# Expert choice one chunk behind its queries, the gate table in 32-token blocks, and other rates for the gathered rows

## The chip, the cores and the metric

The kernel runs on one core of one Trainium2 chip. A core has engines that run side by side and wait for one another by semaphores: PE (TensorE, matmuls, with its weight loads PEld), DVE (VectorE), ACT (ScalarE), POOL (GpSimd) and SP (SyncE); 16 DMA engines carry data between DRAM and the on-chip memory. The metric is the device time of one execution in microseconds (us). Before the change it is 4591.96 us, the median of 3 runs (4589.6 to 4595.62).

## The reference

One layer of a bidirectional encoder on 512 tokens of width 2048, all in float32:

```
h = rms_norm(x); proj = h @ w_in          # 2048 x 19456, split into nine parts
ret = retention(...) @ w_ret_out          # 8 heads, both directions
att = dilated_window_attention(...) @ w_attn_out
x = x + (sigmoid(gate_ret) * ret + sigmoid(gate_att) * att) @ w_out
h2 = rms_norm(x)
x = x + peer_ffn(h2)

# peer_ffn: 8 heads, 2 x 128 keys, 16384 experts of one neuron, 16 of them for each token and head
q = h2 @ w_query                          # 2048 x 2048
s1, s2 = q's two halves against the head's two sets of 128 keys
v1, i1 = top_k(s1, 16); v2, i2 = top_k(s2, 16)
best, pos = top_k(v1[:, None] + v2[None, :], 16)      # over 256 sums
expert = i1[pos // 16] * 128 + i2[pos % 16]; gate = softmax(best)
out = sum over the 128 chosen of gelu(h2 . u[expert]) * gate * v[expert]
```

## The kernel before

Each product of float32 operands is made of three matmuls: every operand is split into a high part (ACT casts it: whi, uh, vh, wh) and a low part (DVE subtracts: wlo, ul, vl, wl). `load_w` (lines 121 to 134) does this for weights: SP loads two slabs of 128 x 512 (`wraw`, four buffers), ACT makes `whi`, DVE `wlo` (three buffers each). `gemm` (lines 136 to 149) runs over such loads for a chunk of 512 output columns.

The 512 tokens are four tiles of 128. Tile 0 is mixed and routed first (part 0), tiles 1 to 3 afterwards (part 1). `mixers` makes retention and attention, `merge` (line 546) the two output projections, `w_out`, the residual x1 and its norm h2. At the end of `merge`, for each of four chunks of 512 columns and each tile, SP loads the input's piece `xr` (three buffers), DVE adds it to the product in x1, SP writes that to DRAM (`x1D`), and ACT squares it for the norm. Then x1 is scaled, PE transposes it, and h2 is split once more. The norm's gains `fgr` are loaded into the same three buffers as xr.

`routing` (line 634) has four chunks of two heads. In a chunk PE makes the queries, transposes them and multiplies them with the transposed keys `skT`; ACT copies the scores to `s12s`; DVE then selects: five instructions for each of 12 rows of scores (MAX, MAX_INDEX, MATCH_REPLACE and two more, in `top16`), the best of 50 sums, and the indices and gates out of them, some 114 instructions for three tiles. `routing_tables` (line 715) loads the keys with their two inner axes swapped and transposes them on PE.

The experts are used in two ways. For tiles 0 and 1 each token's rows are gathered (a unit of 256 steps: 128 rows of u, one for each of a token's choices, then 128 of v). A step is one indirect DMA of 1 MB on POOL's queue (`gr`, three buffers) and one DVE instruction over 128 x 2048 (line 765 or 774). Steps are dealt out by `tick(anchor, rate)`: the rate is added to a credit, and each whole credit uses one row and issues another after the anchor instruction. For tiles 2 and 3 (256 tokens) all 16384 experts are computed. They are 128 blocks of 128, in the code and here called experts for short: `expert_in(n)` (48 matmuls of 256 columns, weights `ur` loaded and split by `load_u`) and `expert_out` (products with v into `psy`). Between the two the activations are multiplied by a dense table of gates.

The table of gates, 128 x 128 experts by 256 tokens, is built on chip from one-hot vectors: for eight tokens DVE makes `oh2` and part of `oh1`, ACT scales four of oh1 by the gates, PE multiplies them (`gg`), ACT copies the products to `Gs`. A block of 64 tokens is 4 MB and goes to DRAM (`GD`); there are four blocks. Later `gate_tile` reads back two experts' gates for all tokens.

The order after the second merge: routing of three tiles, with `begin_dense` (the first 11 experts, `NFIRST`) put before the last chunk's selection; the transposes of the choices (`hkT`) and their way over DRAM; the table, with 12 experts spread over its blocks and one behind; then 16 steps in which only `expert_out` runs, since 24 experts (`NPRE`) are already there; then steps with one `expert_in` and one `expert_out` each. Rows are gathered at a rate of 1.0 for each eight tokens of the table, at 0.7 (`early_rate`) in the first 24 output steps, and at what is left over in the remaining 96.

The order of instructions on each engine is not the order of the code: a scheduler places them ahead of time by the code's order as a priority and by when it estimates operands to be there. Each engine and each queue then runs its list strictly in order.

## Time and profile before

| | |
|---|---|
| median of 3 runs | 4591.96 us |
| profiled execution | 4602.08 us, span 4600.3 us |
| mean granted TensorE clock | 0.967 of full speed |
| PE busy | 4211.8 us (92%) |
| DVE busy | 3439.3 us (75%) |
| ACT, POOL busy | 1917.0 us, 795.5 us |
| moved by DMA | 1358.78 MB, mean 295 GB/s |

The span runs from the first to the last instruction. A busy share is a mean over stages that have different limits, so the rows below go by stages. Matmuls are pipelined and their ends are modelled. A bracket behind a row of a timeline is the idle time of that engine before the instruction, and what ended it. PEclk is the granted clock as a share of 2.4 GHz.

### The profile page before, as it was taken

How to read it: one execution, taken by the hardware profiler on the slowest of the kernel's cores; microseconds unless marked ns; L12 is line 12 of the kernel's file. 1: busy time of each engine (PE TensorE's matmuls, PEld its weight loads, DVE VectorE, ACT ScalarE, POOL GpSimd, SP SyncE). 2: the span in 40 equal slices, each digit the busy share in tenths (PEclk: the TensorE clock that was granted, in tenths of full speed). 3: DMA queues.
4: the chain of work that ended last, by engine and by line, in shares of the span. 5: the costliest groups of instructions: out<-in, count | busy, mean ns of one | idle time of the engine just before them, and what ended most of it. 6: DMA issues, size and time to landing. Idle time of an engine off the chain costs nothing.

```text
span 4600.3 us, 57918 instructions
## 1 busy us (share of the span) xinstructions
PE 4211.8 (92%) x21638; PEld 3524.4 (77%) x21638; DVE 3439.3 (75%) x4495; ACT 1917.0 (42%) x2674; POOL 795.5 (17%) x516
## 2 busy tenths in 40 slices
PE   8999998988998999989979977886799999999999
PEld 6878776765776778767758866786689998899997
DVE  7454554546566878677678878888779998999997
ACT  6444555545442323443432333344434443344443
POOL 0000000000002112222122221012112332344332
PEclk9999999999999999999989998998899999999999
DMA  7666675758658889888899885267889999999997
GB/s 241 226 219 218 215 243 178 244 193 287 224 160 303 323 290 331 313 305 320 300 346 373 340 323 202 92 236 292 318 302 363 397 400 391 401 400 402 405 403 293
DMA packets 510171, 1358.78 MB, mean 295 GB/s; under 512 B 49216, under 2 KB 129088, under 8 KB 440768
## 3 DMA queue, kind: packets, MB, share of 16 engines
q1 hardware_dynamic: 432800, 816.00, 50.9%
q0 software_dynamic: 73728, 536.90, 29.7%
q8 instruction: 170, 2.79, 0.2%
q10 hardware_dynamic: 3360, 2.17, 0.2%
q14 instruction: 113, 0.93, 0.1%
HBM read 1290.05 MB, written 64.88 MB: 295 GB/s over the span
## 4 chain that ended last, share of the span: by engine, by line
PE 50%; DMA 18%; DVE 13%; issue 13%; ACT 3%; POOL 2%; SPq 0%; ACTq 0%; DVEq 0%; POOLq 0%
PE gB L147 9%; PE gB L148 9%; PE gB L146 9%; PE psy L981 3%; PE psy L982 3%; PE psy L980 3%; PE psa L856 3%; PE psa L854 3%; PE psa L855 3%; DMA gr<-in_peer_v,eid 3%; DMA ur<-in_u_feat 3%; DMA wraw<-in_w_in 2%; POOL gr L756 2%; DVE wlo L131 2%; DMA vr<-in_peer_v 2%
## 5 line engine op out<-in xcount | busy, mean ns | idle before, releaser
L131 DVE TENSOR_TENSOR wlo<-wraw,whi 128x1024 fp32r<-128x1024 f32 x752 | 917.2, 1223 | 650.6 <-ACT whi L130 636.0
L130 ACT CAST whi<-wraw 128x1024 fp32r<-128x1024 f32 x752 | 789.4, 1051 | 1227.7 <-PE gB L148 913.6
L756 POOL DMA_INDIRECT gr<-in_peer_u,eid x256 | 362.9, 1418 | 2752.8 <-DVE eid L743 1535.1
L774 DVE SCALAR_TENSOR_TENSOR accg<-gr,wg,accg 128x2048 f32<-128x2048 f32 x256 | 600.5, 2346 | 50.6 <-DMA gr<-in_peer_v,eid 38.5
L765 DVE SCALAR_TENSOR_TENSOR gr<-gr,hrow 128x2048 f32<-128x2048 f32 x256 | 583.8, 2284 | 45.7 <-DMA gr<-in_peer_u,eid 44.2
L854 PE MATMUL psa<-rh,uh 128*128 128x256 f32 x2048 | 582.1, 284 | 29.6 <-ACT uh L839 29.6
L756 POOL DMA_INDIRECT gr<-in_peer_v,eid x256 | 432.4, 1689 | 994.8 <-DVE accg L774 929.1
L856 PE MATMUL psa<-rh,ul 128*128 128x256 f32 x2048 | 581.8, 284 | 9.8 <-DVE ul L840 9.8
L855 PE MATMUL psa<-rl,uh 128*128 128x256 f32 x2048 | 580.0, 283 | 0.0
L839 ACT CAST uh<-ur 128x1024 fp32r<-128x1024 f32 x256 | 268.9, 1051 | 479.0 <-DMA ur<-in_u_feat 381.1
L981 PE MATMUL psy<-vl,wh 128*128 128x512 f32 x1024 | 405.1, 396 | 19.7 <-DVE vl L974 19.5
L854 PEld LDWEIGHTS psa<-rh,uh 128*128 128x128 f32 x2048 | 390.9, 191 | 34.7 <-ACT uh L839 30.5
L980 PE MATMUL psy<-vh,wh 128*128 128x512 f32 x1024 | 402.5, 393 | 6.0 <-ACT vh L973 5.9
L982 PE MATMUL psy<-vh,wl 128*128 128x512 f32 x1024 | 400.7, 391 | 0.0
L855 PEld LDWEIGHTS psa<-rl,uh 128*128 128x128 f32 x2048 | 397.6, 194 | 4.0
L856 PEld LDWEIGHTS psa<-rh,ul 128*128 128x128 f32 x2048 | 390.7, 191 | 12.2 <-DVE ul L840 12.0
L973 ACT CAST vh<-vr 128x1024 fp32r<-128x1024 f32 x256 | 267.9, 1050 | 300.6 <-DMA vr<-in_peer_v 164.5
L974 DVE TENSOR_TENSOR vl<-vr,vh 128x1024 fp32r<-128x1024 f32 x256 | 310.4, 1220 | 76.8 <-ACT vh L973 76.4
L147 PE MATMUL gB<-wlo,rh 128*128 128x512 f32 x768 | 316.3, 412 | 52.3 <-DVE wlo L131 52.0
L840 DVE TENSOR_TENSOR ul<-ur,uh 128x1024 fp32r<-128x1024 f32 x256 | 311.2, 1218 | 57.5 <-ACT uh L839 56.3
L146 PE MATMUL gB<-whi,rh 128*128 128x512 f32 x768 | 309.2, 406 | 31.5 <-ACT rh L570 22.7
L148 PE MATMUL gB<-whi,rl 128*128 128x512 f32 x768 | 311.0, 405 | 0.3 <-DVE rl L571 0.2
(467 smaller groups left out, 7957.5 us busy)
## 6 DMA issues: line engine op xcount, KB each, us to landing
wraw<-in_w_in SPq DMA_DIRECT2D x528, 512.0 KB, 5.0
ur<-in_u_feat SPq DMA_DIRECT2D x256, 512.0 KB, 9.6
vr<-in_peer_v SPq DMA_DIRECT2D x256, 512.0 KB, 9.9
wraw<-in_w_ret_out SPq DMA_DIRECT2D x64, 512.0 KB, 6.1
wraw<-in_w_out SPq DMA_DIRECT2D x64, 512.0 KB, 5.8
wraw<-in_peer_w_query SPq DMA_DIRECT2D x64, 512.0 KB, 4.9
wraw<-in_w_attn_out SPq DMA_DIRECT2D x32, 512.0 KB, 6.8
GD<-Gs SPq DMA_DIRECT2D x4, 4096.0 KB, 14.6
```

What stands on the lines that cost most here:

```text
L130: nc.scalar.copy(whi, raw)
L131: low = nc.vector.tensor_sub(wlo, raw, whi.bitcast(F32))
L146: nc.tensor.matmul(ps[t], ah(k), whi[:, j], start=first, stop=False)
L147: nc.tensor.matmul(ps[t], ah(k), wlo[:, j], start=False, stop=False)
L148: nc.tensor.matmul(ps[t], al(k), whi[:, j], start=False, stop=last)
L756: nc.gpsimd.indirect_dma_start(out=r, out_offset=None, in_=pu if s < P else pv_, in_offset=bass.IndirectOffsetOnAxis(ap=u.eid[:, s % P:s % ...
L765: nc.vector.scalar_tensor_tensor(r, r, 1.0, u.hrow, op0=ALU.mult, op1=ALU.mult, accum_out=u.ag[:, s:s + 1])
L774: nc.vector.scalar_tensor_tensor(u.acc, r, u.wg[:, s - P:s - P + 1], u.acc, op0=ALU.mult, op1=ALU.add)
L854: nc.tensor.matmul(psa[:, j], uh[:, cs], chi[k], start=k == 0, stop=False)
L855: nc.tensor.matmul(psa[:, j], uh[:, cs], clo[k], start=False, stop=False)
L856: nc.tensor.matmul(psa[:, j], ul[:, cs], chi[k], start=False, stop=k == KT - 1)
L981: nc.tensor.matmul(ps[:, t], wh[:, j, ts_], vl[:, j], start=False, stop=False)
```

## The change

`merge` adds the residual into xr itself, writes xr to DRAM, lets ACT square it into x1 and then copy it to x1. `routing` is cut in two: `queries(c)` makes the scores of a chunk, `select(c, scs)` chooses; chunk c's selection follows the queries of chunk c + 1, and the first experts (`before_last`) now come between the last queries and the last two selections. The score tiles have eight buffers for four. The keys are laid out on the host and loaded with one DMA. The scratch tile `ef` goes. The table's blocks are 32 tokens (`TB`), eight of them, with two buffers for Gs; 16 experts come before the table and 7 are spread over it; rows are gathered at 0.6 for each eight tokens of the table and at 1.1 in the first 24 output steps. A gate tile holds four experts.

```diff
--- before.py
+++ after.py
@@ -607,9 +607,10 @@
             for t in range(T):
                 xr = mg.tile([P, 512], F32, name="xr", tag="xr", bufs=3)
                 nc.sync.dma_start(xr, x4[t0 + t][:, cs])
-                nc.vector.tensor_add(x1[t][:, cs], ps[t], xr)
-                nc.sync.dma_start(x1D[t0 + t][:, cs], x1[t][:, cs])
-                nc.scalar.activation(xr, x1[t][:, cs], AF.Square, accum_out=ss4[:, t, c:c + 1])
+                nc.vector.tensor_add(xr, ps[t], xr)
+                nc.sync.dma_start(x1D[t0 + t][:, cs], xr)
+                nc.scalar.activation(x1[t][:, cs], xr, AF.Square, accum_out=ss4[:, t, c:c + 1])
+                nc.scalar.copy(x1[t][:, cs], xr)
         fg = mg.tile([P, KT], F32, name="ffng")
         nc.sync.dma_start(fg, I["ffn_norm_g"][0].rearrange("(k p) -> p k", p=P))
         for t in range(T):
@@ -634,13 +635,12 @@
 
         N2 = 2 * T
         gates, e1, e2 = [rt.tile([P, T, 8, 16], F32, name=n, bufs=1) for n in ("gates", "e1", "e2")]
-        for c in range(4):
+        def queries(c):
+
             ps = paired((I["peer_w_query"][0], c * 512, tiles2))
             qn = rt.tile([P, T, 512], F32, name="qn", bufs=2)
             for t in range(T):
                 nc.scalar.copy(qn[:, t], ps[t])
-            v12 = rt.tile([P, T, 2, 2, 16], F32, name="v12")
-            i12 = rt.tile([P, T, 2, 2, 16], U32, name="i12")
             scs = []
             for i in range(4):
                 pt = bank("qT")
@@ -652,11 +652,14 @@
                 for t in range(T):
                     nc.tensor.matmul(ss[:, t * P:(t + 1) * P], qT[:, t * P:(t + 1) * P], skT[:, 4 * c + i],
                                      start=True, stop=True)
-                sc = rt.tile([P, T * P], F32, name="s12s", bufs=4)
+                sc = rt.tile([P, T * P], F32, name="s12s", bufs=8)
                 nc.scalar.copy(sc, ss[:, :T * P])
                 scs.append(sc)
-            if c == 3 and before_last:
-                before_last()
+            return scs
+
+        def select(c, scs):
+            v12 = rt.tile([P, T, 2, 2, 16], F32, name="v12")
+            i12 = rt.tile([P, T, 2, 2, 16], U32, name="i12")
             for i in range(4):
                 for t in range(T):
                     scr = rt.tile([P, P], F32, name="scr")
@@ -710,19 +713,22 @@
             nc.vector.tensor_mul(gates.rearrange("p t (c u) k -> p t c u k", c=4)[:, :, c],
                                  ex.rearrange("p (t u) k -> p t u k", t=T),
                                  sm.rearrange("p (t u) -> p t u", t=T)[:, :, :, None].to_broadcast([P, T, 2, 16]))
+
+        found = {}
+        for c in range(4):
+            found[c] = queries(c)
+            if c == 3 and before_last:
+                before_last()
+            if c > 0:
+                select(c - 1, found.pop(c - 1))
+        select(3, found.pop(3))
         return e1, e2, gates
 
     def routing_tables(rt):
         tab = rt.tile([P, 3, 16], F32, name="tab", bufs=1)
         nc.sync.dma_start(tab.rearrange("p a b -> p (a b)"), bcast(I["c_rank"], 48))
         skT = rt.tile([P, 16, P], F32, name="skT", bufs=1)
-        for q4 in range(4):
-            sk = rt.tile([P, 4, P], F32, name="sk", bufs=1)
-            nc.sync.dma_start(sk, I["peer_sub_keys"][0].rearrange("h s k d -> k (h s) d")[:, 4 * q4:4 * q4 + 4])
-            ps = bank("skT")
-            for i in range(4):
-                nc.tensor.transpose(ps[:, i * P:(i + 1) * P], sk[:, i], ident)
-            nc.scalar.copy(skT[:, 4 * q4:4 * q4 + 4].rearrange("p a b -> p (a b)"), ps)
+        nc.sync.dma_start(skT, I["key_feat"].rearrange("d (a k) -> d a k", a=16))
         return skT, tab
 
 
@@ -738,9 +744,8 @@
         u.t = t
         u.eid = ga.tile([P, P], I32, name=f"eid{t}")
         u.gate = ga.tile([P, P], F32, name=f"gate{t}")
-        ef = ga.tile([P, P], F32, name="ef", tag="ef")
-        nc.vector.scalar_tensor_tensor(ef, flat(e1), float(P), flat(e2), op0=ALU.mult, op1=ALU.add)
-        nc.vector.tensor_copy(u.eid, ef)
+        nc.vector.scalar_tensor_tensor(u.gate, flat(e1), float(P), flat(e2), op0=ALU.mult, op1=ALU.add)
+        nc.vector.tensor_copy(u.eid, u.gate)
         nc.vector.tensor_copy(u.gate, flat(gates))
         u.h2 = h2row
         gstate["todo"] += [(u, s) for s in range(2 * P)]
@@ -814,13 +819,13 @@
 
     TG = 2
     ND = TG * P
-    TB = 64
+    TB = 32
     NB = ND // TB
     NE = 2
     NV = 8
     NGRP = P // NV
     NPRE = 24
-    NFIRST = 11
+    NFIRST = 16
     NLAST = 1
     right = ctx.enter_context(ExitStack())
     pools = {}
@@ -902,7 +907,7 @@
         for blk in range(NB):
             for n in range(*[NFIRST + (NPRE - NLAST - NFIRST) * (blk + i) // NB for i in (0, 1)]):
                 expert_in(n)
-            Gs = gb.tile([P, P, TB], F32, name="Gs")
+            Gs = gb.tile([P, P, TB], F32, name="Gs", bufs=2)
             for o in range(TB // OB):
                 t0 = blk * TB + o * OB
                 cols = lambda v: v[:, t0:t0 + OB, None].to_broadcast([P, OB, P])
@@ -924,7 +929,7 @@
                         nc.tensor.matmul(ps[:, i * P:(i + 1) * P], oh2[:, j], oh1[:, j], start=True, stop=True)
                     j0 = o * OB + 4 * q
                     nc.scalar.copy(Gs[:, :, j0:j0 + 4], ps.rearrange("p (t e) -> p e t", t=4))
-                tick(last, 1.0)
+                tick(last, 0.6)
             nc.sync.dma_start(GD[blk], Gs)
         for n in range(NPRE - NLAST, NPRE):
             expert_in(n)
@@ -938,15 +943,17 @@
 
     W = {}
 
-    def gate_tile(m):
-        Gt = d2.tile([P, NB, NE * TB], F32, name="Gt")
-        nc.sync.dma_start(Gt, GD[:, :, NE * m:NE * (m + 1), :].rearrange("b p e t -> p b (e t)"))
+    NG = 4
+
+    def gate_tile(i):
+        Gt = d2.tile([P, NB, NG * TB], F32, name="Gt")
+        nc.sync.dma_start(Gt, GD[:, :, NG * i:NG * (i + 1), :].rearrange("b p e t -> p b (e t)"))
         return Gt
 
     def weigh(m, Gt):
         ge = A_out.pop(m)
         gv = ge.rearrange("p j (b t) -> p b j t", t=TB)
-        nc.vector.tensor_mul(gv, gv, Gt.rearrange("p b (j t) -> p b j t", t=TB))
+        nc.vector.tensor_mul(gv, gv, Gt.rearrange("p b (j t) -> p b j t", t=TB)[:, :, m % 2 * NE:(m % 2 + 1) * NE])
         wh = d2.tile([P, NE, ND], F32R, name="wh", bufs=7)
         wl = d2.tile([P, NE, ND], F32R, name="wl", bufs=7)
         nc.scalar.copy(wh, ge)
@@ -954,7 +961,7 @@
         W[m] = (wh, wl)
 
     G0 = NPRE // NV
-    early_rate = 0.7
+    early_rate = 1.1
     left_steps = [(NGRP - 1 - G0) * 8]
 
     def expert_out(g, i):
@@ -998,8 +1005,8 @@
         for q in range(NV):
             n = NV * g + q
             if n < P:
-                if n % NE == 0:
-                    Gt = gate_tile(n // NE)
+                if n % NG == 0:
+                    Gt = gate_tile(n // NG)
                 if n >= NPRE:
                     expert_in(n)
                 if n % NE == NE - 1:
@@ -1018,6 +1025,8 @@
     host = {n: np.ascontiguousarray(inputs[n]) for n in _INS}
     u = host["peer_u"].reshape(P, P, KT, P)
     host["u_feat"] = np.ascontiguousarray(u.transpose(0, 3, 2, 1)).reshape(P, P, KT * P)
+    keys = host.pop("peer_sub_keys").reshape(2 * H, P, P)
+    host["key_feat"] = np.ascontiguousarray(keys.transpose(2, 0, 1)).reshape(P, 2 * H * P)
     host.update(shape_constants())
     return host
```

The first place at which the order changes is SP's queue in the second merge, from the third chunk of `w_out` to the fourth (x1D is the residual in DRAM, DMAHW3_49 and the like are the landing of an earlier DMA of the same queue, Activation_49 and DVE_49 are ACT and DVE). Before:

```order
L611 DMA x1D<-x_0_19291 128x512 [waits DMAHW6_49,DVE_49]
L611 DMA x1D<-x_1_19292 128x512 [waits DVE_49]
L609 DMA xr<-in_x 128x512 [waits Activation_49] x2
L611 DMA x1D<-x_2_19293 128x512 [waits DMAHW2_49,DVE_49]
L127 DMA wraw<-in_w_out 128x2x512 [waits DMAHW3_49,DVE_49]
L609 DMA xr<-in_x 128x512 [waits DMAHW4_49,Activation_49]
L127 DMA wraw<-in_w_out 128x2x512 [waits DMAHW5_49,DVE_49]
```

The same place now:

```order
L611 DMA x1D<-xr 128x512 [waits DMAHW3_49,DVE_49]
L611 DMA x1D<-xr 128x512 [waits DVE_49]
L609 DMA xr<-in_x 128x512 [waits DMAHW3_49,Activation_49]
L611 DMA x1D<-xr 128x512 [waits DVE_49]
L127 DMA wraw<-in_w_out 128x2x512 [waits DMAHW7_49,DVE_49]
L609 DMA xr<-in_x 128x512 [waits DMAHW4_49,DMAHW0_49]
L609 DMA xr<-in_x 128x512 [waits DMAHW6_49,DMAHW1_49,Activation_49]
L127 DMA wraw<-in_w_out 128x2x512 [waits DMAHW2_49,DVE_49]
```

The loads of xr waited for ACT alone or for a DMA eight places back; now each waits for the landing of a write of x1D as well, and the third write and the weight loads stand behind the first of these waits.

The second place is DVE in the second routing, at the weight splits of the second chunk. Before, the end of the first chunk's selection and the first split behind it:

```order
L522 MATCH_REPLACE scr_20861<-best,cand 128x50
L683 COPY di<-i12f 128x6
L684 TENSOR_TENSOR di<-i12f 128x6x15
L523 MAX best<-scr_20861 128x8
L131 TENSOR_TENSOR wlo<-wraw,whi 128x1024
L524 MAX_INDEX pos<-best,scr_20861 128x8
L706 TENSOR_TENSOR ex<-best 128x96
L686 CAST pf<-pos 128x96
```

Now, in the midst of the first chunk's selection (v and i are the values and indices of the first 16):

```order
L524 MAX_INDEX i_20969<-v_20968,scr 128x8
L131 TENSOR_TENSOR wlo<-wraw,whi 128x1024
L779 SCALAR_TENSOR_TENSOR accg<-gr,wg,accg 128x2048
L522 MATCH_REPLACE scr<-v_20968,s12s 128x128
L520 MAX v_20968<-s12s 128x8
L131 TENSOR_TENSOR wlo<-wraw,whi 128x1024
L779 SCALAR_TENSOR_TENSOR accg<-gr,wg,accg 128x2048
L523 MAX v_20968<-scr 128x8
L521 MAX_INDEX i_20969<-v_20968,s12s 128x8
```

Before, 99 instructions of a selection stood ahead of the next chunk's fourth split; now 32 do, and the splits of a chunk are spread through the selection of the chunk before it.

The third place is DVE at the second routing's end. Before, the last split of the last chunk and the start of its selection, whose other instructions then alternate with the first experts' ul:

```order
L703 TENSOR_REDUCE e_20478<-mu 128x3x32
L131 TENSOR_TENSOR wlo<-wraw,whi 128x1024
L520 MAX v_21903<-s12s 128x8 x2
L521 MAX_INDEX i_21904<-v_21903,s12s 128x8
L522 MATCH_REPLACE scr<-v_21903,s12s 128x128
```

Now, 85 instructions of the third chunk's selection behind the last split:

```order
L689 CAST pf<-pos 128x96
L520 MAX v_22911<-s12s 128x8
L698 TENSOR_TENSOR th<-pf,tab 128x1536
L845 TENSOR_TENSOR ul<-ur,uh 128x1024
L699 TENSOR_TENSOR mu<-th,tab 128x1536
L845 TENSOR_TENSOR ul<-ur,uh 128x1024 x2
L700 TENSOR_REDUCE jr<-mu 128x96
```

The end of the third selection and all of the fourth now lie beside the first experts, where the fourth alone did.

## Rows read from the trace of the kernel before

**Rows 1.** Page, parts 1 and 2: PE's share, and granted clock in 40 slices

```profile
PE 4211.8 (92%) x21638; PEld 3524.4 (77%) x21638; DVE 3439.3 (75%) x4495; ACT 1917.0 (42%) x2674; POOL 795.5 (17%) x516
...
PEclk9999999999999999999989998998899999999999
```

**Rows 2.** Stages: length; PE, PEld, DVE, ACT, POOL busy; clock; DMA share; GB/s

```profile
2623.00:2729.00 106.00, 100.95 (x434) 80.85 (x432) 77.25 (x53) 30.88 (x42) 26.70 (x20) 1.00 0.95 360
2729.00:2751.00 22.00, 2.21 (x9) 1.38 (x9) 12.80 (x16) 7.02 (x13) 3.55 (x3) 0.60 0.88 336
...
2797.00:2967.00 170.00, 133.60 (x592) 105.12 (x590) 150.82 (x553) 47.59 (x71) 11.70 (x8) 0.90 0.33 119
2967.00:3032.00 65.00, 62.49 (x530) 61.92 (x531) 58.97 (x178) 30.53 (x34) 1.68 (x1) 0.97 0.58 198
3046.00:3254.00 208.00, 142.29 (x1029) 135.47 (x1028) 181.78 (x273) 100.55 (x220) 51.21 (x31) 0.84 0.72 278
3254.00:3281.00 27.00, 17.92 (x118) 17.23 (x118) 7.72 (x9) 4.87 (x7) 1.14 (x1) 0.81 1.00 377
3281.00:3366.00 85.00, 75.91 (x316) 59.34 (x316) 70.72 (x71) 33.16 (x37) 10.56 (x9) 0.96 0.93 331
3460.00:4560.00 1100.00, 1085.24 (x6968) 986.89 (x6968) 1030.83 (x826) 445.09 (x484) 396.40 (x207) 1.00 1.01 394
```

**Rows 3.** Waits of PE, 2729 to 2797: total us, times, longest

```profile
PE mT L597 <- DVE x L623: 18.3, 2, 16.4
PE skT L724 <- DMA sk<-in_peer_sub_keys: 6.4, 3, 4.4
```

**Rows 4.** DVE's timeline: start and length, then the scaling of x1

```profile
2744.03 1.29 DVE L623 TENSOR_SCALAR x<-x,ssx 128x2048 f32<-128x2048 f32 x1 [4.81 <-DMA x1D<-x]
2749.07 1.29 DVE L623 TENSOR_SCALAR x<-x,ssx 128x2048 f32<-128x2048 f32 x1 [3.75 <-DMA wraw<-in_peer_w_query]
```

**Rows 5.** Waits of PE, 2797 to 2967

```profile
PE gB L147 <- DVE wlo L131: 33.7, 6, 9.3
```

**Rows 6.** The table's writes (line 928): us from issue to landing

```profile
DMA to landing us min/median/max: 13.8/14.6/16.0
```

**Rows 7.** ACT's timeline: a copy of 512 columns; first scores of two chunks

```profile
2798.61 0.59 ACT L641 COPY qn<-gB 128x512 f32<-128x512 f32 x1 [0.32 <-PE gB L148]
...
2804.42 0.48 ACT L656 COPY s12s<-s 128x384 f32<-128x384 f32 x1 [1.15 <-PE s L653]
...
2962.86 0.48 ACT L656 COPY s12s<-s 128x384 f32<-128x384 f32 x1 [1.02 <-PE s L653]
```

**Rows 8.** DMA, 2620 to 2750: POOL's queue; issues, KB, us to landing

```profile
q0 software_dynamic: 3584, 26.08, 50.3%
...
x1D<-x SPq DMA_DIRECT2D x12, 256.0 KB, 11.9
```

**Rows 9.** Waits of PE, 985 to 1020 (first merge)

```profile
PE skT L724 <- DMA sk<-in_peer_sub_keys: 10.6, 3, 8.5
```

**Rows 10.** DVE by line, 2797 to 3046: busy us, mean ns | idle before

```profile
L131 DVE TENSOR_TENSOR wlo<-wraw,whi 128x1024 fp32r<-128x1024 f32 x23 | 27.8, 1212 | 8.1 <-ACT whi L130 8.1
L774 DVE SCALAR_TENSOR_TENSOR accg<-gr,wg,accg 128x2048 f32<-128x2048 f32 x8 | 18.8, 2347 | 1.6 <-DMA gr<-in_peer_v,eid 1.6
```

**Rows 11.** DVE by line, 3046 to 3254

```profile
L765 DVE SCALAR_TENSOR_TENSOR gr<-gr,hrow 128x2048 f32<-128x2048 f32 x29 | 66.1, 2283 | 6.4 <-DMA gr<-in_peer_u,eid 5.1 <-DMA hrow<-h2D 1.3
...
L840 DVE TENSOR_TENSOR ul<-ur,uh 128x1024 fp32r<-128x1024 f32 x21 | 25.1, 1219 | 19.8 <-ACT uh L839 19.8
```

**Rows 12.** The reads of gate tiles (line 943): us to landing

```profile
DMA to landing us min/median/max: 4.1/8.9/12.6
```

**Rows 13.** Waits of PE, 3460 to 4560

```profile
PE psy L981 <- DVE vl L974: 12.1, 9, 5.0
PE psa L856 <- DVE ul L840: 2.5, 1, 2.5
```

## The prediction

> **What bounds the kernel now.** I read the page first: PE is busy for 92% of the span, and its clock row falls below full speed only around slices 17 to 29 [rows 1]. Then I cut the span into stages [rows 2]. The last long one, 3460 to 4560 us, has PE at 1085.2 of 1100 us at the full clock (2.4 GHz): PE sets its time there, and DVE (1030.8) and the DMA engines (share 1.01) have next to nothing to spare [rows 2]. What is slack lies between 2729 and 3281 us. In the first stretch PE does 2.2 us of work in 22 [rows 2]; it waits for the scaled residual [rows 3], which waits for the residual's own write to DRAM [rows 4]. Then come the transposed keys: PE waits 6.4 us for their loads [rows 3]. From 2797 to 2967 DVE is busy 150.8 of 170 us, PE 133.6 [rows 2], and all that PE waits for there is wlo, 33.7 us [rows 5]: the second half of each weight split stands on DVE behind a chunk's whole selection. From 3046 to 3254 (the gate table) DVE is busy 181.8 of 208 us and PE 142.3 at a granted clock of 0.84 [rows 2]: DVE sets the pace. From 3254 to 3281 the last 4 MB of the table go to DRAM and come back [rows 2, 6]. So PE sets the time, except where DVE holds it back in two stretches and a DMA in three.
>
> All sums stand against the profiled execution: span 4600.3 us, 4602.1 us with what lies around it. The median of the runs shown is 4592.0, that is 10.1 less; I carry the difference over to it.
>
> **Residual and squares (merge).** The add now writes xr, which goes to DRAM itself, and x1 is a second copy. DVE's scaling no longer waits for the write: 4.8 and 3.75 us go (the second is put down to a weight load, but the tile's own write is still out) [rows 4]. Into the chain come the ACT copies, three of 512 columns, 0.59 us by the like copy [rows 7], 1.8 in all. That is -8.6 + 1.8 = **-7**, ends -9 and 0. The price stands on SP: xr is loaded again from a ring of three, and that load now waits for the landing of the residual's write, with the next weight loads behind it on the queue; the third write is itself behind the first wait. I count seven such landings in series, one after the first chunk and two after each of the other three. One landing takes 11.9 us here [rows 8], so the bound is 83 us. The other end is 0: half of the bytes in this stretch are rows on POOL's own queue [rows 8], the engines are at a share of 0.95 [rows 2], and holding back SP's loads only changes whose bytes go first, as long as some are queued. I take **+8**, near the lower end, since PE's row there is 101 of 106 us [rows 2] and loads for several steps lie ready in the raw and split buffers. The Trainium skill (DMA: Bandwidth & Descriptors, Anatomy of one DMA) gives a DMA about 2.0 us fixed and its bytes at 436 GB/s; by that estimate 256 KB land in 2.6 us and seven landings are 18 us, so the term would be about +2 and the time 4544. The trace says 11.9, because the rings are full, and the trace is used.
>
> **Keys.** Eight strided loads, 32 transposes and eight copies go; one load of 1 MB each time stands in SP's queue ahead of the need. Before the second routing 6.4 us of waits [rows 3] and about 4 us of PE's transposes and their ACT round go: **-10** (ends -4 and -14). Before the first merge the wait reads 10.6 us [rows 9], but the merge's own first operands load in the same stretch and would be waited for next: **-3** (0 to -10).
>
> **Selection one chunk later.** Score tiles double to eight; each chunk's selection now follows the next chunk's projection. In the new DVE order five of the eight splits come after about 32 of some 114 selection instructions, with the rest behind them. From chunk 1's first scores to chunk 4's is 158.4 us [rows 7]; without the 33.7 us of waits PE needs 124.7. DVE's work in the same piece: a selection is (150.8 - 27.8 - 18.8) / 3 = 34.7 us, as the window holds three [rows 2, 10]; two of them, 21 splits of 1.21 and 7 row updates of 2.35 make 111 us. DVE is under PE, so the wait falls away but for blocks of 54 and 67 selection instructions (13 and 20 us) against three split buffers: I leave 6 and take **-28** (ends -34 and 0).
>
> **Five more experts before the table.** 530 matmuls took 65 us [rows 2], so 48, one expert, 5.9 us, and five **+29.5** (ends 28 and 31). They cover what remained of the selection, now two chunks: 2 x 34.7 + 34 splits of 1.22 = 111 us of DVE, against 16 x 5.9 + some 20 us of tail on PE. That is even, so +3 for the order in which DVE meets them (0 to +12).
>
> **The table.** 32 steps at 0.6 instead of 1.0 issue 12.8 rows fewer: 12.8 x 2.283 = 29.2 us of DVE [rows 11]. By the new order six experts instead of ten stand among its products: 8 splits x 1.219 = 9.8 [rows 11]. DVE paces the stage, so **-39** (ends -49, if the 19.8 us of waits for uh [rows 11] shrink as well, and -10, if the chain from DVE over ACT and PE to the next buffer paces it instead). Two blocks in flight also take away ACT's wait for the 4 MB write, which lies in that span already. At the end 2 MB stand where 4 MB landed in 14.6 us, half at the same rate [rows 6]; the first tile read back is twice as large, against 8.9 us now [rows 12]: -7.3 + 2.3 = **-5** (ends -9 and +4).
>
> **Rows given back.** In the output-only stretch 16 steps at 1.1 instead of 0.7 add 6.4 rows: 14.6 us of DVE on 70.7 of 85 [rows 2], and 6.7 MB on 28.1 (85 us at 331 GB/s), which at the 394 GB/s of the last stage need 88 us. Ends 0 and +15; **+8**, the middle, as two engines become full at once. The last stage gets 256 - 19.2 - 26.4 = 210.4 rows where it had 207.2: 7.3 us of DVE where PE waits for it 14.6 us in all [rows 13]: **+2** (0 to 7). Gate tiles for four experts carry the same bytes in half the loads; 0.
>
> **Sum:** -7 + 8 - 10 - 3 - 28 + 29.5 + 3 - 39 - 5 + 8 + 2 = -41.5: 4602.1 becomes 4560.6, and on the median's level 4592.0 becomes **4550**.
>
> **The rivals.**
> *SP's queue decides (slower).* In the second merge six of the seven landings, 71 us at 11.9 each, reach PE in full: the raw ring runs dry, since SP waits and not a transfer. For it: ACT already waits there for weights, and the landings are long [rows 8]. Against it: the share of 0.95, which tells that bytes and not issue are short. -41.5 - 8 + 71 = +21.5, 4613. It makes the change slower than before once more than about 50 us, or four landings, are exposed. The Trainium skill (DMA: Bandwidth & Descriptors, Anatomy of one DMA) says that a semaphore wait is held on the issuing sequencer before dispatch, which is the mechanism.
> *DVE decides the routing.* The 28 us are not won, because DVE's blocks of selection keep PE's splits back as before, while the five experts cost in full: 4578. For it: DVE at 89% there [rows 2]. Against it: 111 us of work against 125.
> *PE's clock decides the table.* With four experts fewer among the products PE runs at 1.2 GHz throughout. Its work there is 142.3 x 0.84 = 120 us at full speed, less 4 x 5.9 = 96, at half speed 192 us instead of the 169 that DVE needs: +23, 4573. For it: the granted clock was 0.84 there and 0.60 between 2729 and 2751 [rows 2], after PE had idled; it was 1.00 where PE ran without pause. Against it: at 68% busy it still held 0.84. The Trainium skill (TensorE: Matmul & The Clock Gate, HAM oscillation) has idle gaps drop the clock; the rows agree, but not that it would fall for the whole stage.
> *All cover holds.* Rows and landings cost nothing, the uh waits shrink: -41.5 - 8 - 8 - 10 = 4524.
>
> **How the numbers follow.** Forecast 0.58 (own range 4530 to 4572), DVE in the routing 0.14, clock 0.08, all cover 0.10, SP's queue 0.10. The range is 4515 to 4590: it leaves out SP's queue and a little at each end. About 0.2% (9 us) is what a measurement can tell from no change. Faster by more: the forecast, the clock and the full cover, and most of the routing rival, 0.86; within it 0.05; slower 0.09, nearly all of it SP's queue.
>
> **What would show it.** After: PE's first transpose of x1 some 12 us after the merge's last matmul, not 16.4; no wait for sk; in the four chunks a wait for wlo under 10 us; some 40 us from one chunk's scores to the next; the table in about 169 us; the output-only stretch 85 to 100 us with DVE near full. I am wrong if PE waits for weights in the second merge by more than 20 us, if the table stays over 190 us, or if the last stage grows by over 10.

## The result, and the profile after

The changed kernel takes 4558.97 us (median of 4, 4555.0 to 4564.9), the kernel before 4593.79 beside it: ratio 0.9923, 95% interval 0.9904 to 0.9941. The forecast was 4550, with a range of 4515 to 4590. The profiled execution takes 4557.7 us against 4602.1, 44.4 less; the forecast sum was -41.5. The sum held, but several of its terms did not: the two largest errors, in the table and in the last stage, cancel, and that is luck.

Of the profile after, the stages as in [rows 2] (length; PE, PEld, DVE, ACT, POOL busy; granted clock; DMA share; GB/s): behind the second merge, the four chunks, the table, the last stage.

```profile
2730.00:2752.00 22.00, 5.40 (x23) 4.10 (x22) 15.20 (x24) 11.04 (x23) 5.04 (x3) 0.67 0.92 351
2790.00:2925.00 135.00, 120.14 (x557) 96.94 (x555) 131.02 (x524) 42.33 (x63) 7.80 (x7) 0.96 0.42 152
3033.00:3184.00 151.00, 109.81 (x804) 104.59 (x804) 144.43 (x241) 89.85 (x209) 34.84 (x19) 0.88 0.75 275
3399.00:4519.00 1120.00, 1095.63 (x6967) 992.62 (x6966) 1036.62 (x832) 446.12 (x483) 387.99 (x210) 0.99 1.01 390
```

The four chunks and the table are shorter, the last stage is longer. Between the same instructions in both traces (us, worked out from their starts and ends; one execution of each kernel):

| stretch | before | after | difference | forecast |
|---|---|---|---|---|
| second merge's last matmul to last x1 transpose | 34.5 | 32.1 | -2.4 | -7 |
| from there to the first scores | 40.9 | 29.7 | -11.2 | -10 |
| first scores of chunk 1 to those of chunk 4 | 158.4 | 128.0 | -30.4 | -28 |
| chunk 4's scores to the first `hkT` | 69.5 | 99.2 | +29.7 | +32.5 |
| table, first one-hot to last copy into Gs | 207.1 | 151.9 | -55.2 | -39 |
| from there to the first output matmul | 27.9 | 24.9 | -3.0 | -5 |
| 16 output-only steps | 111.5 | 117.7 | +6.2 | +8 |
| last stage, 12th to last `yacc` | 1131.4 | 1151.6 | +20.2 | +2 |

**Behind the second merge.** PE's waits, 2730 to 2770 (total us, times, longest; against [rows 3]), then DVE's:

```profile
PE mT L597 <- DVE x L624: 11.0, 1, 11.0
PE mT L597 <- DVE rl L568: 5.6, 1, 5.6
```

```profile
DVE x L631 <- DMA fgr<-in_ffn_norm_g: 5.3, 1, 5.3
DVE rl L568 <- ACT rh L567: 3.5, 5, 1.6
```

The scaling no longer waits for the residual's write [rows 4], and PE's first wait ends at 11.0 us, as forecast. But the gain row `fgr` shares xr's ring, which now waits for that write to land; its multiplication stands on DVE ahead of the low halves `rl`, and holds them for 5.3 us. A wait went and another came, in one line further down. The 5.3 us are the longest case: in eight more profiles with this merge the wait is 4.3 us or shorter, and the stretch to the last x1 transpose takes 26.9 to 31.7 us, where this profile has 32.1. The writes themselves land sooner than in [rows 8] (DMA issues, 2620 to 2750; KB, median us to landing):

```profile
x1D<-xr SPq DMA_DIRECT2D x12, 256.0 KB, 8.4
```

The merge's last product (the 576 matmuls with `w_out`) was forecast 8 us longer, for those landings. From its first matmul to its last it takes 140.5 us, before 143.2. PE's waits in it are 5.1 us before (2620 to 2729; none ahead of that) and 3.3 us after (2590 to 2730), so hardly a landing reached PE:

```profile
PE gB L147 <- DVE wlo L131: 2.1, 3, 0.8
PE gB L146 <- DVE x L610: 1.8, 1, 1.8
PE gB L146 <- ACT whi L130: 1.2, 2, 0.8
```

```profile
PE gB L146 <- ACT whi L130: 1.4, 1, 1.4
PE gB L146 <- DVE xr L610: 1.1, 1, 1.1
PE gB L147 <- DVE wlo L131: 0.8, 1, 0.8
```

**Keys.** PE waits for no `sk`. In the first merge another load took its place, PE's waits from 980 to 1020 (against [rows 9]):

```profile
PE gB L146 <- ACT rh L570: 15.5, 3, 12.2
PE gB L146 <- ACT ah L570: 1.3, 1, 1.3
PE gB L148 <- DVE rl L571: 0.5, 1, 0.5
```

The merge's first operands stand on SP behind the 1 MB of keys: the longest wait is 12.2 us where it was 8.5. By the same matmuls of the products in both traces, the changed kernel is 4 to 6 us late behind that merge (1100 to 1200 us) and 0.8 us late from 1700 to 1840: the loss is hidden by then. At 2579 us it is 4.0 us late again; why is not shown.

**The four chunks.** PE's waits, 2790 to 2925: of the 33.7 us for `wlo` [rows 5] 10.5 are left, at most 4.6 at once.

```profile
PE gB L147 <- DVE wlo L131: 10.5, 3, 4.6
```

**The table.** DVE by line, 3033 to 3184 (busy us, mean ns | idle before; against [rows 11]), and the landing of its eight writes (against [rows 6]):

```profile
L770 DVE SCALAR_TENSOR_TENSOR gr<-gr,hrow 128x2048 f32<-128x2048 f32 x17 | 38.7, 2282 | 5.1 <-DMA hrow<-h2D 5.1
...
L845 DVE TENSOR_TENSOR ul<-ur,uh 128x1024 fp32r<-128x1024 f32 x13 | 15.3, 1216 | 0.0
```

```profile
DMA to landing us min/median/max: 7.2/9.3/12.4
```

17 u rows instead of 29, 13 splits instead of 21, and the 19.8 us of waits for `uh` gone. DVE is busy 144.4 of 151 us: it is still the bound, with next to no pauses.

**The last stage.** PE's waits, 3399 to 4519 (against [rows 13]):

```profile
PE psy L988 <- DVE vl L981: 23.0, 12, 3.3
PE psy L987 <- ACT vh L980: 1.1, 1, 1.1
```

PE waits 24.1 us instead of 14.6, and is busy 1095.6 us instead of 1085.2 over the same matmuls. The second 10 us come with the first: at six places between 3460 and 4460 us, none of which the trace before has, the granted clock falls to half (1.2 GHz) at the end of such a wait or within 1.3 us behind it. PE's busy time at half the clock in this stage, halved, is 11.8 us after and 1.8 before, so the falls account for the longer busy time. One of them, first the waits in the 18 us up to it, then the windows of the wait and behind it:

```profile
POOL gr L761 <- DVE gr L770: 12.4, 4, 7.4
ACT uh L844 <- DMA ur<-in_u_feat: 5.1, 2, 4.0
ACT vh L980 <- DMA vr<-in_peer_v: 3.8, 1, 3.8
DVE vl L981 <- ACT vh L980: 3.4, 1, 3.4
PEld psy L988 <- DVE vl L981: 2.6, 1, 2.6
PE psy L988 <- DVE vl L981: 2.2, 1, 2.2
```

```profile
3560.00:3563.00 3.00, 0.76 (x5) 0.45 (x4) 3.00 (x4) 1.04 (x1) 0.11 (x1) 1.00 0.99 415
3563.00:3567.00 4.00, 4.00 (x12) 3.08 (x12) 4.00 (x3) 0.00 (x0) 0.00 (x0) 0.57 1.01 406
```

Read from the third row down (the first two are not part of it): a load that is late (DMA share 1.01) holds ACT, ACT holds DVE's `vl`, DVE holds PE for 2.2 us (PE is busy for 0.76 of 3 us), and PE then works at a granted clock of 0.57 over the next 4. The other five follow waits of 1.8 to 3.3 us, one of them in two pieces of 1.1 and 0.8. The Trainium skill (TensorE: Matmul & The Clock Gate, HAM oscillation) tells of the clock dropping behind a matmul loop's waits for DMA; this window shows such a drop, behind a wait for DVE that a late load caused. Not every wait of this length costs the clock: two of the eight in that stretch, 2.5 us up to 3745 and 2.7 us up to 4118, are followed by full clock, and so are three of 1.5 to 2.5 us between 3902 and 3946 in the trace before. The first of the two, the wait and what is behind it:

```profile
3743.00:3746.00 3.00, 0.59 (x3) 0.51 (x4) 3.00 (x4) 1.31 (x2) 0.00 (x0) 1.00 1.00 408
3746.00:3750.00 4.00, 4.00 (x19) 3.31 (x18) 4.00 (x5) 0.13 (x1) 0.00 (x0) 1.00 1.01 410
```

What decides between the two is not shown.

### The profile page after: what moved, and what is told of

It reads as the page before. It is cut to its first block, busy times and chain, and to the rows that moved or that the text cites. A ratio compares the mean times of both kernels' runs of the same rounds, so it can differ in the third digit from the quotient of the medians.

```text
span 4555.9 us, 57795 instructions
## 1 busy us (share of the span) xinstructions
PE 4214.7 (93%) x21606; PEld 3528.1 (77%) x21606; DVE 3436.7 (75%) x4495; ACT 1923.3 (42%) x2682; POOL 793.2 (17%) x516
## 4 chain that ended last, share of the span: by engine, by line
PE 40%; issue 22%; DMA 17%; DVE 13%; POOL 5%; ACT 3%; SPq 0%; POOLq 0%; DVEq 0%; ACTq 0%
PE gB L147 9%; PE gB L148 9%; PE gB L146 9%; POOL gr L761 5%; DMA gr<-in_peer_v,eid 4%; DVE wlo L131 2%; DMA wraw<-in_w_in 2%; DVE accg L779 2%; DVE gr L770 2%; PE psy L988 2%; DMA gr<-in_peer_u,eid 2%; DMA vr<-in_peer_v 2%; PE psy L989 2%; DMA ur<-in_u_feat 2%; PE psy L987 2%
## 5 line engine op out<-in xcount | busy, mean ns | idle before, releaser
L845 DVE TENSOR_TENSOR ul<-ur,uh 128x1024 fp32r<-128x1024 f32 x256 | 310.9, 1218 | 28.1 <-ACT uh L844 27.9
```

## The experiments

All start from the changed kernel (written "after"). Open were the last stage, what the table's gain is made of, and the two waits that came in the merges. The executions of one kernel scatter by up to 1% (early15: 4537 to 4584), so single edits are read from stage lengths as well; the kernel before ran beside them at 4592.2, 4598.9 and 4593.4 us. The changed kernel itself did not run beside them again, so their medians can be set against its 4559 us only through the ratios to before. Its 0.9923 may be on the high side: eight of the twelve kernels have lower ratios, among them tail_back, which was expected to be slower by 18 us or more. Its profile is also the slowest up to the routing: in seven others with the same instructions up to there the last x1 transpose ends at 2742 to 2759 us, in its own at 2762.5 (before 2763.6). The last stage in all of them (rows that DVE uses there; tokens in a block and experts in a gate tile; length between the 12th and the last `yacc`; PE's waits and busy time in it up to some 32 us before the end):

| kernel | rows | block, tile | length | PE waits | PE busy |
|---|---|---|---|---|---|
| before | 207 | 64, 2 | 1131.4 | 14.6 | 1085.2 |
| tail_back | 207 | 64, 2 | 1127.3 | 10.7 | 1085.2 |
| rates_back | 207 | 32, 4 | 1146.7 | 21.5 | 1094.4 |
| blocks_back | 210 | 64, 2 | 1145.2 | 23.1 | 1090.7 |
| best | 210 | 64, 2 | 1142.7 | 20.0 | 1090.9 |
| gate4_64 | 210 | 64, 4 | 1145.1 | 22.7 | 1091.3 |
| after | 210 | 32, 4 | 1151.6 | 24.1 | 1095.6 |
| sel_same_nf11 | 210 | 32, 4 | 1151.4 | 25.4 | 1094.4 |
| front2 | 210 | 32, 4 | 1153.5 | 26.0 | 1095.8 |
| merge_back | 210 | 32, 4 | 1174.8 | 38.8 | 1104.0 |
| gate2 | 210 | 32, 2 | 1156.6 | 28.7 | 1095.9 |
| early15 | 201 | 32, 4 | 1131.7 | 17.1 | 1083.7 |
| no_fetch | 210 (189 fetched) | 32, 4 | 1136.6 | 17.3 | 1087.6 |
| no_use | 189 (210 fetched) | 32, 4 | 1194.0 | 57.1 | 1104.8 |

Waits and busy time together make up the length, less those 32 us, in every line, and busy time, for the same matmuls, grows with the waits (early15 has 56 matmuls fewer behind its 12th `yacc`). Each line is one execution.

**rates_back**

```diff
-                tick(last, 0.6)
+                tick(last, 1.0)
-    early_rate = 1.1
+    early_rate = 0.7
```

> The changed kernel with the two row rates as before (1.0 a table step instead of 0.6, 0.7 an output step instead of 1.1); blocks, gate tiles, routing and merge stay changed. 12.8 rows go back into the table, 9.6 rows leave the output steps, and the last stage has 207.2 rows again instead of 210.4. Both theories: the table takes 12.8 x 2.28 = 29 us more (151 to about 180), since DVE is busy 144 of 151 us there; the 16 output-only steps go from 116.5 to about 110. Theory A, the last stage is 20 us longer than before because of its 3.2 extra rows on a nearly full DVE: it falls back to about 1132 us, and the time is 4559 + 29 - 6 - 20 = 4562. Rival B, it is longer because of the gate tiles and blocks: it stays at about 1150, and the time is 4582.

4564.4 us (ratio 0.9949, 0.9930 to 0.9968). Its table:

```profile
3018.00:3199.00 181.00, 115.97 (x807) 109.80 (x808) 173.13 (x266) 90.46 (x209) 52.53 (x31) 0.83 0.82 308
```

181.5 us from the first one-hot to the last copy, 29.6 more than after: the rows are worth in the table what was forecast (29.2). The last stage goes back by 5 us only, to 1146.7: rival B by the stage. The time is near theory A's 4562, but it does not decide for A: in its profile the stretches ahead of the routing are 13 us shorter than in that of after, with the same code.

**blocks_back**

```diff
-    TB = 32
+    TB = 64
-            Gs = gb.tile([P, P, TB], F32, name="Gs", bufs=2)
+            Gs = gb.tile([P, P, TB], F32, name="Gs")
-    NG = 4
+    NG = 2
```

> The changed kernel with the table in four blocks of 64 tokens, one block buffer and gate tiles of two experts, as before; the rates, the routing and the merge stay changed. Both theories: ACT waits again some 12 us for the write of a 4 MB block, so the table goes from 151 to about 160, and the way from the last block's copy to the first output matmul from 25.5 to 28.5. Theory A (rows make the last stage longer): the last stage stays at about 1150 us, and the time is 4559 + 12 = 4571. Rival B (gate tiles or blocks make it longer): the last stage is about 1132 us, and the time is 4552.

4538.2 us (0.9885, 0.9863 to 0.9906), not slower than after. In its profile (4563.3, the longest of its five) the table takes 162.5 us (ACT waits 8.4 for the block's write), the last stage 1145.2: between the theories.

**gate2**

```diff
-    NG = 4
+    NG = 2
```

> The changed kernel with gate tiles of two experts instead of four; the table stays in 32-token blocks, so a piece that a load reads is 256 bytes instead of 512. Theory A (rows make the last stage longer): nothing changes there, 1150 us, time 4559. Rival B1 (the doubled gate load holds up the loads behind it): last stage about 1132, time 4540, and the first gate tile lands earlier (about 2 us less before the first output matmul). Rival B2 (pieces of 256 bytes cost DMA time): last stage longer than 1155, time over 4565.

4548.1 us (0.9903, 0.9884 to 0.9922); last stage 1156.6. B1 falls by the stage: smaller gate loads don't give its time back. Theory A (no change from 1151.6) and rival B2 (over 1155) can't be told apart by 5 us in one execution; the time is below what either expected.

**early15**

```diff
-    early_rate = 1.1
+    early_rate = 1.5
```

> The changed kernel with 1.5 rows per output step of the first three groups instead of 1.1: 6.4 rows more in the 16 output-only steps, 3.2 in the next 8, and 9.6 fewer in the last stage (200.8). Theory A (DVE's rows make the last stage longer, 3.2 rows were worth 20 us or a good part of it): the last stage falls to 1132 us or below, the output-only steps go from 116.5 to about 116.5 + 6.4 x 2.28 = 131 at most, time 4555 or less. Rival B (not the rows): the last stage stays within 5 us of 1150 and the time goes to about 4570.

4552.9 us (0.9930, 0.9903 to 0.9956). The last stage falls by 20 us to 1131.7, so rows do lengthen it. But the steps up to the 8th `yacc` take 153.3 us instead of 117.7 (with some 160 matmuls more among them), and from the first output matmul to the end it is 14 us longer in all, with the same rows there: rows are not free in the output-only steps at that rate.

**tail_back** has the edits of rates_back and blocks_back together.

> The changed kernel with everything from the table on as before: blocks of 64 tokens with one buffer, gate tiles of two experts, both row rates as before; 16 experts before the table, the routing and the merge stay changed. The table then holds 12.8 rows more and waits for the 4 MB write: with 181 us (rates back) and 162 us (blocks back) against 151 measured, about 190. Theory A, the part from the first output matmul to the end, 1342.7 us in the changed kernel's profile against 1315.4 before, is longer because of its own edits (rows and gate table): it is 1315 to 1320 here, and the time is 4559 + 40 + 3 - 25 = 4577. Rival B, most of these 27 us is scatter between executions, which the profiles of the variants so far show in the mixers too (1522 to 1546 us for the same instructions): it is about 1330 or more, and the time 4590.

4553.5 us (0.9900, 0.9880 to 0.9920). From the first output matmul to the last `yacc` it takes 1310.8 us, the last stage 1127.3: theory A by the stage; its time, 4577, was missed by 23. The table takes 183.3. From the first one-hot to the first output matmul it takes 212.1 us, after 176.8. So of the 35 us that the rates and blocks win up to there, 32 are given back behind, and the time is not above that of after. Against before, this profile is 44.5 us shorter: 23.8 in the table, which differs by five experts fewer, 11.2 behind the x1 transposes (keys), 5.3 ahead of them and 4.5 from the first output matmul on. The last stage:

```profile
3425.00:4521.00 1096.00, 1085.15 (x6961) 988.10 (x6960) 1029.69 (x824) 447.19 (x482) 395.21 (x207) 1.00 1.02 395
```

**sel_same_nf11**

```diff
-            if c > 0:
-                select(c - 1, found.pop(c - 1))
-        select(3, found.pop(3))
+            select(c, found.pop(c))
-    NFIRST = 16
+    NFIRST = 11
```

> The changed kernel with the routing as before: each chunk's selection ahead of the next projection, 11 experts before the table instead of 16; merge, keys, rates, blocks stay changed. From the second routing's first scores to the first transposed table row the two versions take the same time by the traces of before and after (158.4 + 69.5 = 227.9 and 128.0 + 99.2 = 227.2 us), so what the shift brought can only stand in the table. Theory A: the five experts moved out of it are worth what they cost PE or DVE there: the table goes from 152 to 162 (8 splits x 1.22 us more on DVE) or up to 182 (if the splits' waits of 19.8 us come back), time 4569 to 4590. Rival B: the table's gain was all rows and blocks: it stays within 5 us of 152 and the time within 5 of 4559.

4567.5 us (0.9938, 0.9920 to 0.9955). PE's waits in the four chunks, and DVE's splits in the table:

```profile
PE gB L147 <- DVE wlo L131: 33.4, 6, 9.3
```

```profile
L843 DVE TENSOR_TENSOR ul<-ur,uh 128x1024 fp32r<-128x1024 f32 x23 | 27.1, 1218 | 10.1 <-ACT uh L842 10.1
```

The 33.4 us are back, and still the stretch from the first scores to `hkT` is the same (228.7 and 227.2 us). The table takes 165.7 us, against 147 to 155 in the seven profiles with 32-token blocks, 16 experts and 0.6 rows a step (150.7 on average): theory A by the stage; its time, 4569 at least, is missed by 2 us. The late selection pays for five experts, and these are missing in the table: ten splits, 11.8 us, and the waits for `uh`.

**merge_back**

```diff
-                nc.vector.tensor_add(xr, ps[t], xr)
-                nc.sync.dma_start(x1D[t0 + t][:, cs], xr)
-                nc.scalar.activation(x1[t][:, cs], xr, AF.Square, accum_out=ss4[:, t, c:c + 1])
-                nc.scalar.copy(x1[t][:, cs], xr)
+                nc.vector.tensor_add(x1[t][:, cs], ps[t], xr)
+                nc.sync.dma_start(x1D[t0 + t][:, cs], x1[t][:, cs])
+                nc.scalar.activation(xr, x1[t][:, cs], AF.Square, accum_out=ss4[:, t, c:c + 1])
```

> The changed kernel with the merge's residual as before: the add writes x1, x1 itself goes to DRAM, the squares go into the loaded tile. Theory A (the traces of before and after: 2.3 us won between the second merge's last matmul and its last transposed part, 1.2 us lost in its last product): the way from merge to keys is 2 us longer, the last product 1 us shorter, and the time within 5 us of 4559. Rival B (the new ring's landings cost more than that: with the residual's write out of the ring the second merge runs at least 5 us shorter): time 4552 or less. Rival C (the wait for the write is back in full, 7 us as forecast): 4566 or more.

4549.6 us (0.9884, 0.9867 to 0.9902). DVE's waits behind the merge:

```profile
DVE x L623 <- DMA x1D<-x: 8.0, 2, 5.9
DVE rl L568 <- ACT rh L567: 3.4, 5, 1.3
```

The wait for the write is back, and the stretch to the last x1 transpose takes 35.0 us, against 26.9 to 32.1 in the nine profiles with after's merge (29.4 on average): the edit is worth some 5 us in its stretch. The median doesn't show it, and is 9 us lower (18 by the ratios). That is rival B's time, but not its mechanism: the merge's last product takes 141.9 us, no shorter than with the ring's landings (138.1 to 143.5 in the nine). Why the time is lower stays open. Its profiled execution, 4575 us, has 38.8 us of waits in the last stage with code as in after: so large is the scatter there.

**front2**

```diff
-            fgr = mg.tile([P, 512], F32, name="fgr", tag="xr", bufs=3)
-            nc.sync.dma_start(fgr, bcast(I["ffn_norm_g"][0][cs], 512))
+            fgr = mg.tile([P, T, 512], F32, name="fgr", tag="sg", bufs=2)
+            nc.sync.dma_start(fgr[:, 0], bcast(I["ffn_norm_g"][0][cs], 512))
...
-        skT, tab = routing_tables(rt)
         h2, row, tiles2 = merge(0, mg, [(mg, 0, 1)])
         nc.sync.dma_start(h2gD, row)
+        skT, tab = routing_tables(rt)
```

> The changed kernel with two edits to its loads: the gain rows for the merge's last step go into the gate's free buffers, not into the ring that waits for the residual's landing; and the first routing's keys are loaded behind the first merge instead of ahead of it. Theory A (the gain row's load is what holds DVE for 5.3 us in the second merge, and with it PE): from the second merge's last matmul to its last transposed part 27 us instead of 32, and the first merge's first wait falls from 12.2 to about 8.5 us; since the first merge's 6 us were gone by the second mixer's end, the time is 4559 - 5 = 4554. Rival B: behind that load DVE waits for the splits' first halves anyway, the stage stays at 32, time 4559.

4542.5 us (0.9878, 0.9859 to 0.9897). PE's waits behind the second merge, all of them, and in the first merge:

```profile
PE mT L597 <- DVE x L624: 11.8, 1, 11.8
```

```profile
PE gB L146 <- ACT rh L570: 10.9, 3, 8.1
PE gB L146 <- ACT ah L570: 1.3, 1, 1.3
PE gB L148 <- DVE rl L571: 1.0, 2, 0.5
```

Both waits went as theory A said: 25.9 us to the last x1 transpose, and 8.1 for 12.2. The time is some 12 us below its 4554; the two waits don't account for that.

**no_fetch and no_use** (the first edit is in the issue of a gather, the second in its use; each leaves 21 terms out of the output, no_fetch with the row fetched before in their place)

```diff
-        r = ga.tile([P, D], F32, name="gr", tag="gr", bufs=3)
+        if u.t == 1 and s >= P and (s - P) % 6 == 5:
+            gstate["rows"].append((u, s, gstate["old"]))
+            return
+        r = gstate["old"] = ga.tile([P, D], F32, name="gr", tag="gr", bufs=3)
```

```diff
+            if u.t == 1 and (s - P) % 6 == 5:
+                continue
             nc.vector.scalar_tensor_tensor(u.acc, r, u.wg[:, s - P:s - P + 1], u.acc, op0=ALU.mult, op1=ALU.add)
```

> The changed kernel, in which 21 of the 128 value rows of the second gather unit, all in the last stage, are not fetched; DVE does the same updates on the row fetched before (so these 21 terms of the output are left out of what is computed rightly). 21 x 1.05 MB = 22 MB less for the DMA engines, 57 us at the 389 GB/s of that stage. Theory A (the DMA engines, at a share of 1.00, set the last stage's time together with PE): the stage falls from 1152 us towards what PE needs there, 1096 of 1120 us busy, so to about 1127, and PE's waits for vl shrink. Rival B (DVE sets it): it stays within 5 us of 1152.

> The changed kernel, in which the same 21 value rows are fetched and DVE's update with them is left out (those 21 terms are missing from the output). 21 x 2.3 us = 48 us less of DVE in the last stage, all bytes stay. Theory A (the DMA engines set it): the stage stays within 5 us of 1152 at the same 389 GB/s. Rival B (DVE sets it): it falls to about 1127, where PE is full.

no_fetch 4535.1 us (0.9874, 0.9857 to 0.9891), last stage 15 us shorter; with 22 MB less the DMA engines are at 0.98 and PE waits 17.3 us: theory A, though the stage stays above its 1127. no_use 4590.1 us (0.9994, 0.9979 to 1.0009), last stage 42 us longer, which no theory had. Its waits, 3391 to 4552:

```profile
POOL gr L761 <- DMA gr<-in_peer_v,eid: 111.9, 22, 9.9
...
DVE accg L781 <- DMA gr<-in_peer_v,eid: 78.2, 20, 8.6
```

A row that nobody reads is released by its landing alone, so POOL issues the next gather late, and DVE, in order, stands 78.2 us (13.1 in after) ahead of PE's splits. The edit made a wait of its own, and does not tell DVE's work from the DMA engines'. So DVE's share in the last stage is not settled.

**best and gate4_64**: best is front2 with the edits of blocks_back; gate4_64 the same with `NG = 4`.

> The two load edits of front2 with the table in 64-token blocks, one block buffer and gate tiles of two experts; rates, routing and merge as changed. If the two gains add (4542 with the load edits, 4538 with the old blocks, 4559 with neither), 4525 to 4535; the last stage near 1140 us. Rival (the differences among these medians are scatter): about 4545.

> The same kernel as best, but with gate tiles of four experts (512 KB a load, in pieces of 1 KB). Theory A (the doubled gate load is what takes the DMA rate of the last stage from 392 to 395 down to 389 GB/s): the last stage is about 8 to 15 us longer than in best, and so is the time. Rival B (the 32-token blocks do it, or neither): the last stage is within 5 us of that of best.

4536.1 us (0.9887, 0.9870 to 0.9904) and 4543.3 (0.9899, 0.9880 to 0.9917). The last stages are 1142.7 and 1145.1: the larger gate tile alone costs nothing that shows, so rival B holds. The gains of the single edits don't add up; best has the lowest median of the kernels that compute the whole output, 57 us below the kernel before beside it (4593.4), but can't be told from front2 or blocks_back.

## Why the prediction was right, and where it was wrong

- **Keys, routing, experts, output-only steps** came within 3 us each. The routing and its experts are worth nothing up to `hkT` (-0.7) and 15 us in the table with the new rates and blocks, as sel_same_nf11 shows; with the old ones it is 23.8 (tail_back against before).
- **Second merge's product, forecast +8, measured -2.7.** Of the 83 us of landings counted in series hardly any reached PE: its waits there are 3.3 us, before 5.1. The end of the term's bounds at nothing was the right one, and a landing took 8.4 us, where the prediction worked with 11.9 and set an estimate of 2.6 beside it.
- **x1, forecast -7, measured -2.4 (-5.1 on average of nine profiles).** The step that failed is "DVE's scaling no longer waits for the write: ... -8.6 + 1.8": right for that wait, but it did not ask what else waits for the landing. The ring that was followed to xr's next load also holds `fgr`. front2 takes that wait away and gets 25.9 us, 8.6 below before. So the wait is worth 3.5 us on average, and 6 in the profile of after.
- **First merge, forecast -3.** The rule named there, that the next operand would be waited for, held, and its longest wait is 3.7 us longer than the one that went; hidden by 1700 us.
- **Table, forecast -39, measured -55.** Rows 29.6 (forecast 29.2) by rates_back; the experts 15 instead of 9.8, since the waits for `uh` shrank (the forecast's far end, -49, counted these); 32-token blocks about 7 (157.2 on average of blocks_back, best and gate4_64 against 150.7), counted at nothing in the forecast. The three are single edits against after; in another order they weigh otherwise (the rates 21 us with the old blocks, tail_back against blocks_back).
- **Last stage, forecast +2, measured +20.** The step that failed: "7.3 us of DVE where PE waits for it 14.6 us in all". It priced the 3.2 rows by DVE alone and left out that the DMA engines were at 1.01 in [rows 2]: 3.2 x 1.05 MB at 394 GB/s are 8.5 us of a full resource. no_fetch shows the DMA part. It also took a wait at its own length; here the waits cost about as much again by the clock (+9.5 waits, +10.4 busy). And "Gate tiles ... 0" was wrong for the blocks: at 207 rows 32-token blocks take 1146.7 where 64-token blocks take 1127.3 and 1131.4, at 210 rows about 1152 to 1157 (without merge_back) where 64-token blocks take 1143 to 1145. Each number is one execution, and merge_back (1174.8) shows how far one can lie off; but all six with 32-token blocks are longer than the 64-token ones with the same rows. Why they are is open: the gate tile's size is not it (gate4_64), the pieces read are 512 bytes in both, and the DMA engines move 388 to 390 GB/s (merge_back 382) instead of 392 to 395 at much the same share.

"I am wrong ... if the last stage grows by over 10" came true, and the total was right all the same, by luck: the table gained 16 more than forecast. Taken together, rates and blocks gained nothing that the times show (tail_back): what the change is worth lies in the keys, the late selection with the experts that it pays for, and x1. None of the rivals that are slower came: the second merge's waits for weights are 2.2 us, the 28 us of the routing were won, and the table's clock rose from 0.84 to 0.88. Of the full cover two parts came, the landings at no cost and the shorter waits for `uh`; the third, rows at no cost, did not.

## What to carry to other kernels

Work that is moved into a stage where DMA engines, DVE and PE are all near full is priced by each of them, here by its bytes first, and by what PE's clock loses behind the waits. When a wait for a landing is taken from one instruction, list everything else that uses the same ring of buffers: the wait moves to the next user, and in-order queues carry it to others. Where executions scatter by half a per cent, compare stage lengths over many profiles before a part of the change is given the credit.

## What was not expected of the hardware

- Six of eight waits of PE of 1.8 to 3.3 us in the last stage were followed by some us at half the granted clock, two of 2.5 and 2.7 us were not; PE's busy time there runs from 1085 us (before and tail_back, with 15 and 11 us of waits) to 1105 (no_use, 57 us) for the same matmuls.
- Much of the scatter between executions goes with the clock, though which of the two makes the other is not shown: blocks_back took 4527 us at a mean granted clock of 0.974 and 4563 at 0.968.
- One core moved 395 GB/s for 1.1 ms with its DMA engines at a share of 1.02. The Trainium skill (HBM Reference, Specifications (TRN2)) gives about 358 GB/s as a core's share and about 425 for a core that streams alone; the measured rate lies between.
